# Choosing the weight pieces of the adding DMA by a count of the DMA engines' time instead of by fixed shares

## The chip, the cores and the metric

The kernel runs on one core of one Trainium2 chip. The metric is the device time of one execution in microseconds (us); several executions are timed and their median is given. Beside the times there is one profiled execution, whose trace holds every instruction of TensorE (PE, with its weight loads as PEld), VectorE (DVE), ScalarE (ACT), GpSimd (POOL) and SyncE (SP), and every transfer.

## The reference

The input is one sequence of 256 rows of 1024 numbers (float32). Two blocks of two layers each follow. Cut to what matters:

```python
def first_block(x, ...):
    for l in range(2):
        x = hybrid_layer(x, ...)
    return rmsnorm(x, final_norm_g)

def hybrid_layer(x, ...):
    proj = einsum("bsd,de->bse", rmsnorm(x, norm_g), w_in)          # 1024 x 3584
    (a_u, a_v, a_z, b_b, b_c, b_x, b_z, c_q, c_k, c_v, c_z, d_q, d_k, d_v, d_z) = split(proj)
    y_a = conformer_conv(a_u, a_v, ...) * silu(a_z)                 # 31-wide conv, layernorm, silu
    y_b = short_gated_conv(b_b, b_c, b_x, ...) * silu(b_z)          # 3-wide conv
    y_c = window_gqa(c_q, c_k, c_v, swa_sink) * silu(c_z)           # sliding-window attention
    y_d = neighborhood_attn(d_q, d_k, d_v, na_rpb) * silu(d_z)      # 2-D attention with a bias
    return x + einsum("bse,ed->bsd", concatenate([y_a, y_b, y_c, y_d]), w_out)

def second_block(x, ...):
    for i in range(2):
        x = x + 0.5 * _swiglu(_rmsnorm(x), ffn1_w_gate[i], ffn1_w_up[i], ffn1_w_down[i])
        x = x + _mixing(_rmsnorm(x), w_in[i], w_out[i], ...)        # two attentions and a recurrence
        x = x + 0.5 * _swiglu(_rmsnorm(x), ffn2_w_gate[i], ffn2_w_up[i], ffn2_w_down[i])
    return _rmsnorm(x, final_norm)
```

The four feed-forward networks have 1024 x 2816 gate and up matrices and a 2816 x 1024 down matrix each. All products are wanted at nearly float32 precision.

## The kernel before

**Weights and their halves.** All weights come once from memory, in 206 chunks, most of them 128 x 2048 float32 (1 MB, 16 tiles of 128 x 128, in the order in which PE uses them). A chunk is loaded into one of three buffers `st` by SP's queue (`weight_loads`). The matrix products run in fp32r, a faster form with fewer bits, so each weight is split into `hi` (the weight rounded to fp32r) and `lo` (what the rounding left), with three buffers of each; a product of the activation (split alike) with a weight tile is three matmuls. PE has two kinds of tile: in the "T" tiles (lines 563 to 565, `MM3`) the weight tile is loaded three times for 256 columns each; in the "W" tiles (lines 576, 577 and 579, `MMW`) it is two matmuls, of 512 columns with `hi` and 256 with `lo`.

**How a piece is split.** `weight_splits` takes each chunk in two halves ("pieces"; the first two chunks in four). ACT copies the piece to `hi` (profile: L472, hi<-st). Then `lo` is made in one of two ways: DVE subtracts (L495, lo<-st,hi), or ACT copies -hi into `lo` (L472, lo<-hi) and POOL issues a DMA that adds `st` onto it (L592, lo<-st), with no work for DVE. When the last piece of a chunk is done, its `st` goes back to the loads and `nprep`, the number of chunks split, is raised. `at` is the number of chunks that PE's tasks have taken. Which way a piece goes is decided before by a fixed share of the pieces in each kind of stage (line 451 and lines 628 to 630): 0.25 in the feed-forward stages (`SHARE_F`), 0.6 in the mixing stages of block 1 (`SHARE_A`), 0.45 in those of block 2 (`SHARE_B`). A counter `owed` grows by the share with every piece, and a piece that brings it to 1 is an add, from chunk 3 on (`FAST`).

**Who sets the order.** The program has no loops on the chip. In the build, `Scheduler.step` runs the tasks (generators) greedily: each pending operation has a cost in a small table of durations, each engine a clock (P, A, V, G, and D for SP's loads), each dependence between engines a latency (`LAT`); the operation with the least start time less a weighted priority goes next, onto the end of its engine's instruction stream. So the planner's numbers fix the static order of every engine, and on the chip the engines wait for each other by semaphores. Clock D is charged for a load with its bytes over 360e3 per us (`DMA`, whose duration is `nbytes / 360e3`). For an add, `DMAadd` charges POOL 1.2 us for the issue and puts the result 4.0 us later (`ADD_LATE`); D is not charged.

**Stages.** In time there are eight: the two mixing layers of block 1 (A0, A1; function `mix_a`), then for each layer of block 2 a feed-forward stage, a mixing stage (B0, B1; `mix_b`) and a feed-forward stage (ffn1 to ffn4). A feed-forward stage is 33 chunks, 528 tiles. A mixing stage A is two chunks for the values (v0, v1), then 13 groups of projections in the order a_v, a_u, b_c, c_z, c_q, c_k, d_z, d_q, b_z, b_x, d_k, b_b, a_z (a chunk each, c_k half a one; T tiles), then the output projection (4 chunks, W tiles) over y. Chunk 3 is a_u, chunk 4 b_c, chunk 6 c_q. Behind a_u, DVE makes `hp` and from it `ca`, the 31-wide convolution, in 62 steps, and a layernorm follows: PE sums over the channels (`ca,ones`), ACT takes the mean, DVE subtracts it, and so on, up to `a_z` and the first two row groups of y. The second attention (`na`, twice) begins with the scores (`dk,dq` on PE) and the bias step of the softmax on DVE (L526), which needs the bias `nb`, gathered by eight SP transfers of 96 KB from `rpb` (task `biases`, per mixing layer). The short convolution is `bp` and `bc`. The first y groups that the output projection wants are those of the two attentions, its last those of the two convolutions.

## Time and profile before

| | |
|---|---|
| median of 3 runs | 1361.81 us (1359.84, 1361.81, 1370.74) |
| the profiled execution | 1359.77 us, span of its instructions 1358.0 us, mean granted TensorE clock 0.978 |
| PE busy | 1277.9 us, 94% (weight loads 1144.4 us, 84%) |
| DVE busy | 865.0 us, 64% |
| ACT busy | 921.3 us, 68% |
| POOL busy | 320.1 us, 24% |
| HBM | 217.94 MB read, 1.05 MB written |

The span runs from the first to the last instruction of the profiled execution; 1.8 us of its time lie around it. A matmul's end is modelled and matmuls overlap their weight loads, so a busy PE isn't PE at its peak; the granted clock (PEclk, 1.00 is the higher of TensorE's two levels, 2.4 GHz, and 0.50 the lower, 1.2 GHz) says at which speed it ran. "DMA share" is the mean busy share of the core's 16 DMA engines. The stages are read from the trace at A0 4 to 152 us, A1 152 to 290, ffn1 290 to 478, B0 478 to 634, ffn2 634 to 820, ffn3 820 to 1006, B1 1006 to 1160, ffn4 1160 to 1358. In a row of a group or of the timeline, "bank<-act,hi" is what an instruction writes and reads, [5.84 <-DMA lo<-st] how long it stood before and what it waited for; "xN" the number of instructions.

### The profile page before, as it was taken

How to read it: one execution, taken by the hardware profiler on the slowest of the kernel's cores; microseconds unless marked ns; L12 is line 12 of the kernel's file. 1: busy time of each engine (PE TensorE's matmuls, PEld its weight loads, DVE VectorE, ACT ScalarE, POOL GpSimd, SP SyncE). 2: the span in 40 equal slices, each digit the busy share in tenths (PEclk: the TensorE clock that was granted, in tenths of full speed). 3: DMA queues.
4: the chain of work that ended last, by engine and by line, in shares of the span. 5: the costliest groups of instructions: out<-in, count | busy, mean ns of one | idle time of the engine just before them, and what ended most of it. 6: DMA issues, size and time to landing. Idle time of an engine off the chain costs nothing.

```text
span 1358.0 us, 21863 instructions
## 1 busy us (share of the span) xinstructions
PE 1277.9 (94%) x8530; PEld 1144.4 (84%) x8530; DVE 865.0 (64%) x1481; ACT 921.3 (68%) x1420; POOL 320.1 (24%) x318
## 2 busy tenths in 40 slices
PE   6899988999999999789999999999999888999997
PEld 5888887888888898678888888888899776888886
DVE  6586658569966556856666556666555785666632
ACT  5487748777686578587666656666559767766652
POOL 4222312242121112512222112222121340322211
PEclk9899998999999999899999999999999899999998
DMA  8887988798777779255877777777778645877771
GB/s 262 229 234 203 231 237 232 204 241 271 224 235 240 236 219 256 82 171 156 263 233 234 228 230 228 225 240 237 239 232 230 180 104 161 236 243 242 236 226 53
DMA packets 59783, 294.09 MB, mean 217 GB/s; under 512 B 12448, under 2 KB 14240, under 8 KB 34208
## 3 DMA queue, kind: packets, MB, share of 16 engines
q1 hardware_dynamic: 39232, 219.01, 45.3%
q0 software_dynamic: 20448, 73.69, 28.5%
q8 instruction: 67, 1.10, 0.3%
q14 instruction: 36, 0.29, 0.1%
HBM read 217.94 MB, written 1.05 MB: 161 GB/s over the span
## 4 chain that ended last, share of the span: by engine, by line
PE 70%; ACT 10%; DVE 7%; DMA 7%; issue 3%; POOL 2%; SPq 0%; POOLq 0%; DVEq 0%; ACTq 0%
PE bank L576 34%; PE bank L577 19%; PE bank L579 4%; DMA lo<-st 3%; DVE sp L495 3%; ACT hi L472 3%; DMA st<-ws 3%; PE bank L563 2%; PE bank L565 2%; PE bank L564 2%; ACT lev L472 2%; PE bank L535 2%; ACT lo L472 1%; PE bank L546 1%; ACT pt L472 1%
## 5 line engine op out<-in xcount | busy, mean ns | idle before, releaser
L576 PE MATMUL bank<-act,hi 128*128 128x512 f32 x1456 | 520.0, 395 | 2.3 <-DVE act L495 2.3
L472 ACT ACTIVATE hi<-st 128x1024 fp32r<-128x1024 f32 (+3 forms) x416 | 428.6, 1036 | 80.6 <-DMA st<-ws 39.2
L577 PE MATMUL bank<-act,lo 128*128 128x256 f32 x1664 | 433.4, 281 | 0.6 <-ACT act L472 0.6
L495 DVE TENSOR_TENSOR lo<-st,hi 128x1024 fp32r<-128x1024 f32 (+1 forms) x274 | 338.0, 1237 | 133.5 <-ACT hi L472 130.1
L577 PEld LDWEIGHTS bank<-act,lo 128*128 128x128 f32 x1664 | 312.8, 188 | 18.6 <-ACT act L472 0.9
L576 PEld LDWEIGHTS bank<-act,hi 128*128 128x128 f32 x1456 | 273.6, 188 | 57.8 <-DVE act L495 3.8
L592 POOL DMA_DIRECT2D lo<-st x142 | 123.9, 873 | 652.2 <-ACT lo L472 524.1
L576 PE MATMUL bank<-ha,hi 128*128 128x512 f32 x672 | 236.7, 394 | 0.0
L565 PE MATMUL bank<-act,lo 128*128 128x256 f32 x720 | 208.9, 290 | 24.9 <-DMA lo<-st 24.9
L563 PE MATMUL bank<-act,hi 128*128 128x256 f32 x720 | 214.1, 297 | 0.0
L564 PE MATMUL bank<-act,hi 128*128 128x256 f32 x720 | 207.7, 288 | 0.0
L577 PE MATMUL bank<-ha,lo 128*128 128x256 f32 x704 | 192.7, 281 | 0.0
L565 PEld LDWEIGHTS bank<-act,lo 128*128 128x128 f32 x720 | 141.7, 197 | 26.1 <-DMA lo<-st 26.1
L472 ACT ACTIVATE lo<-hi 128x1024 fp32r<-128x1024 f32 (+1 forms) x142 | 149.3, 1052 | 3.8
L576 PEld LDWEIGHTS bank<-ha,hi 128*128 128x128 f32 x672 | 126.2, 188 | 27.0
L563 PEld LDWEIGHTS bank<-act,hi 128*128 128x128 f32 x720 | 142.1, 197 | 5.9 <-issue 5.0
L564 PEld LDWEIGHTS bank<-act,hi 128*128 128x128 f32 x720 | 141.4, 196 | 0.1
L577 PEld LDWEIGHTS bank<-ha,lo 128*128 128x128 f32 x704 | 132.4, 188 | 2.7
L495 POOL TENSOR_TENSOR fs<-fs,rbc 128x512 f32<-128x512 f32 x44 | 64.0, 1456 | 179.4 <-ACT fs L472 179.4
L495 DVE SCALAR_TENSOR_TENSOR x<-bank,x 128x256 f32<-128x256 f32 x128 | 53.6, 422 | 58.6 <-PE bank L579 56.7
L495 DVE TENSOR_TENSOR fh<-bank,fh 128x256 f32<-128x256 f32 x88 | 37.1, 423 | 76.6 <-ACT fh L472 76.6
L579 PE MATMUL bank<-act,hi 128*128 128x512 f32 x208 | 82.2, 395 | 0.1
(216 smaller groups left out, 1543.8 us busy)
## 6 DMA issues: line engine op xcount, KB each, us to landing
st<-ws SPq DMA_DIRECT2D x197, 1024.0 KB, 5.0
lo<-st POOLq DMA_DIRECT2D x136, 512.0 KB, 5.7
st<-ws SPq DMA_DIRECT2D x2, 1040.0 KB, 7.1
st<-ws SPq DMA_DIRECT2D x4, 512.0 KB, 7.4
st<-ws SPq DMA_DIRECT2D x8, 192.0 KB, 5.3
nb<-rpb SPq DMA_DIRECT2D x16, 96.0 KB, 7.5
st<-ws SPq DMA_DIRECT2D x2, 768.0 KB, 6.5
lo<-st POOLq DMA_DIRECT2D x2, 520.0 KB, 6.7
```

The lines of the kernel that those rows point to most:

```text
L472: return Op([("A", dur, lambda: self.nc.scalar.activation(out, in_, func, **kw))], outs, ins, ACT_SETS.get(func))
L495: return (eng, dur, lambda: fn(out, *ins, **kw)), [extent(a) for a in aps]
L535: return Op([("P", dur, lambda: self.nc.tensor.matmul(out, lhsT, rhs, start=start, stop=stop))], [extent(out)], [extent(lhsT), extent(rhs)])
L546: mm(o, l, r, start=st, stop=sp)
L563: mm(out, ah, bh, start=first, stop=False)
L564: mm(out, ah, bl, start=False, stop=False)
L565: mm(out, al, bh, start=False, stop=last)
L576: mm(out, wh, x, start=first, stop=False)
L577: mm(out[:, 0], wl, x[:, 0], start=False, stop=False)
L579: mm(out, wh, x, start=False, stop=True)
L592: return Op([("G", ADD_ISSUE, lambda: self.nc.gpsimd.dma_start(out, src, accum_op=ALU.add))], [extent(out)], [extent(src), extent(out)], l ...
```

## The change

`owed`, `share` and the three fixed shares go. In their place the planner now charges an add to clock D as well: an operation has `moves`, the free size of the piece times `ADD_RATE` (2.7e-3 us for each of 1024 elements of a partition, so 2.76 us), which begins when both D and POOL's issue are done and moves D on; the result is there 1.9 us after that (`ADD_LATE`). A piece becomes an add when three things hold at the moment its `hi` copy has been placed: the chunk is 3 or later, as before; at least one chunk more has been split than PE's tasks have taken (`nprep > at`); and the planner's clock D is not ahead of ACT's (`c["D"] <= c["A"]`).

```diff
@@ -206,18 +206,16 @@
 PRIO = dict(w1=0.8, w2=-1.8, w3=0.4, epilogue=0.5, gate=1.7, up=1.5, rstd=2.0, norm=1.3, values=0.7,
             conv=0.3, att=1.8, evac=1.1, level=0.3, prep=-0.7, rec=2.3, bias=-1.3, vg=0.2)
 ADD_ISSUE = 1.2
-ADD_LATE = 4.0
-SHARE_F = 0.25
-SHARE_A = 0.6
-SHARE_B = 0.45
+ADD_LATE = 1.9
+ADD_RATE = 2.7e-3
 WEIGH = dict(P=0.0118, A=0.7, V=0.35, G=0.1681, D=1.0)
 
 
 class Op:
-    __slots__ = ("ways", "outs", "ins", "tset", "dep", "gen", "late")
-
-    def __init__(self, ways, outs, ins, tset=None, late=0.0):
-        self.ways, self.outs, self.ins, self.tset, self.late = ways, outs, ins, tset, late
+    __slots__ = ("ways", "outs", "ins", "tset", "dep", "gen", "moves")
+
+    def __init__(self, ways, outs, ins, tset=None, moves=0.0):
+        self.ways, self.outs, self.ins, self.tset, self.moves = ways, outs, ins, tset, moves
 
 
 class Event:
@@ -385,7 +383,10 @@
         w[2]()
         end = start + cost
         self.clock[eng] = end
-        self.commit(op, eng, end + op.late)
+        if op.moves:
+            self.clock["D"] = end = max(self.clock["D"], end) + op.moves
+            end += ADD_LATE
+        self.commit(op, eng, end)
         t.op = None
         self.advance(t)
         return True
@@ -448,7 +449,6 @@
         self.used = 0
         self.nprep = 0
         self.at = 0
-        self.share = self.owed = 0.0
 
 
     def A(self, out, in_, func, scale=1.0, bias=0.0, accum_out=None):
@@ -590,7 +590,7 @@
     def DMAadd(self, out, src):
 
         return Op([("G", ADD_ISSUE, lambda: self.nc.gpsimd.dma_start(out, src, accum_op=ALU.add))],
-                  [extent(out)], [extent(src), extent(out)], late=ADD_LATE)
+                  [extent(out)], [extent(src), extent(out)], moves=free_n(src) * ADD_RATE)
 
     def split(self, hi, lo, src):
         yield self.A(hi, src, AF.Copy)
@@ -625,9 +625,8 @@
                 s = slice(j * n // parts, (j + 1) * n // parts)
                 yield self.loaded[i][j]
                 yield self.A(hi[:, s], st[:, s], AF.Copy)
-                self.owed += self.share
-                self.owed, on_pool = (self.owed - 1.0, True) if self.owed >= 1.0 else (self.owed, False)
-                if on_pool and i >= FAST:
+                c = self.s.clock
+                if i >= FAST and self.nprep > self.at and c["D"] <= c["A"]:
                     yield self.A(lo[:, s], hi[:, s].bitcast(F32), AF.Copy, scale=-1.0)
                     yield self.DMAadd(lo[:, s].bitcast(F32), st[:, s])
                 else:
@@ -952,7 +951,6 @@
                 yield nxt["summed"][KT - 1]
                 done.done = True
 
-            self.share = SHARE_F
             s.spawn(self.rstd(st, "copy"), PRIO["rstd"])
             if extra is not None:
                 s.spawn(extra, 0.0)
@@ -1274,7 +1272,6 @@
                 yield nxt["summed"][KT - 1]
                 done.done = True
 
-            self.share = SHARE_A
             s.spawn(self.rstd(st, "both"), PRIO["rstd"])
             s.spawn(norm(), PRIO["norm"])
             s.spawn(self.free_rows(st, True))
@@ -1694,7 +1691,6 @@
                 yield nxt["summed"][KT - 1]
                 done.done = True
 
-            self.share = SHARE_B
             s.spawn(self.rstd(st, "normed"), PRIO["rstd"])
             s.spawn(norm(), PRIO["norm"])
             s.spawn(self.free_rows(st, False))
```

The build gives these numbers of adds on POOL, by stage:

| | A0 | A1 | ffn1 | B0 | ffn2 | ffn3 | B1 | ffn4 | all |
|---|---|---|---|---|---|---|---|---|---|
| before | 20 | 22 | 18 | 15 | 18 | 16 | 15 | 18 | 142 |
| changed | 7 | 10 | 18 | 13 | 19 | 20 | 14 | 26 | 127 |

The first add is in chunk 3 (a_u, both halves) before and in chunk 6 (c_q, its first half) in the changed kernel. In the feed-forward stages most chunks have an add in one half; before it is mostly the first half, in the changed kernel mostly the second.

The orders of the engines change with it. Where a buffer's name carries a number, the number is the buffer's alone.

On SP, in the front of A0, the order before; `st` is a weight chunk, `nb` the bias of the second attention, `msk` a mask that is needed late:

```order
L587 DMA st_73<-ws 128x2048
L587 DMA nb<-rpb 64x6x64 x3
L587 DMA st_71<-msk 128x384
L587 DMA nb<-rpb 64x6x64 x5
L587 DMA st_71<-ws 128x2048
```

and in the changed kernel:

```order
L587 DMA st_73<-ws 128x2048
L587 DMA st_71<-ws 128x2048
L587 DMA st_72<-msk 128x384
L587 DMA nb<-rpb 64x6x64 x8
L587 DMA st_72<-ws 128x1024
```

The load of chunk 6 (the `st_71<-ws` row) stood behind the eight gathers and now stands ahead of them.

On ACT, at the same place, the order before; hi_75 and lo_78 are chunk 4, hi_76 and lo_79 chunk 5, hi_74 and lo_77 chunk 6, and a row lo<-hi is the negated copy of an add:

```order
L472 ACTIVATE hi_75<-st_72 128x1024 x2
L472 ACTIVATE lo_78<-hi_75 128x1024
L472 ACTIVATE hi_76<-st_73 128x1024 x2
L472 ACTIVATE lo_79<-hi_76 128x1024
L472 ACTIVATE hi_74<-st_71 128x1024
L472 ACTIVATE lo_77<-hi_74 128x1024
```

and in the changed kernel (act is the activation, xnt a normed row group on the way into it):

```order
L472 ACTIVATE hi_75<-st_72 128x1024
L472 ACTIVATE act_81<-xnt_88 128x2x256
L472 ACTIVATE hi_75<-st_72 128x1024
L472 ACTIVATE act_81<-xnt_89 128x2x256
L472 ACTIVATE hi_76<-st_73 128x1024 x2
L472 ACTIVATE hi_74<-st_71 128x1024
L472 ACTIVATE lo_77<-hi_74 128x1024
```

The negated copies of chunks 4 and 5 are gone; that of chunk 6's first half stays and is the first of the program.

On PE, at the end of A0's projections, the order before; dk and dq are the second attention's operands, and rows L563 to L565 are a T tile of a projection:

```order
L546 MATMUL bank_120<-dk,dq 128x256
L546 MATMUL bank_123<-dk,dq 128x256
L563 MATMUL bank_117<-act_81,hi_75 128x256
L564 MATMUL bank_117<-act_81,hi_75 128x256
L565 MATMUL bank_117<-act_81,lo_78 128x256
```

and in the changed kernel (rows L576 and L577 are a W tile of the output projection; ca, th and dg belong to the convolution's layernorm):

```order
L565 MATMUL bank_118<-act_81,lo_79 128x256
L576 MATMUL bank_119<-act_80,hi_74 128x512
L577 MATMUL bank_119<-act_80,lo_77 128x256
L535 MATMUL bank_123<-ca,ones 128x256 x2
L576 MATMUL bank_119<-act_80,hi_74 128x512
L577 MATMUL bank_119<-act_80,lo_77 128x256
L535 MATMUL bank_123<-ones,th_159 128x1 x4
L535 MATMUL bank_123<-dg_114,ones 128x128
L535 MATMUL bank_123<-dg_115,ones 128x128
L546 MATMUL bank_122<-dk,dq 128x256
L546 MATMUL bank_121<-dk,dq 128x256
```

Before, 61 T tiles stand behind ca,ones and 37 behind the last of the scores (dk,dq); in the changed kernel both stand behind the last T tile, with one W tile ahead of ca,ones and one behind it. In A1 of the changed kernel half of the scores stands ahead of the last 33 T rows and the other half has 8 tiles behind it.

## Rows read from the trace of the kernel before

**Rows 1.** DMA queues of the page: packets, MB, share of 16 engines' span
```profile
q1 hardware_dynamic: 39232, 219.01, 45.3%
q0 software_dynamic: 20448, 73.69, 28.5%
```

**Rows 2.** Busy time by stage: A0, A1, ffn1, B0 and ffn4
```profile
core 0: us, PE busy (x) PEld busy (x) DVE busy (x) ACT busy (x) POOL busy (x), PEclk, DMA share, GB/s
4.00:152.00 148.00, 128.06 (x906) 117.75 (x906) 105.34 (x232) 101.24 (x173) 45.06 (x56) 0.95 0.87 237
152.00:290.00 138.00, 123.74 (x900) 114.88 (x899) 91.06 (x218) 97.38 (x161) 33.40 (x41) 0.96 0.88 226
290.00:478.00 188.00, 187.28 (x1082) 164.06 (x1081) 135.39 (x226) 131.80 (x190) 40.62 (x43) 1.00 0.78 242
478.00:634.00 156.00, 137.63 (x1205) 126.72 (x1204) 103.39 (x175) 114.86 (x198) 43.54 (x32) 0.96 0.61 168
...
1160.00:1358.00 198.00, 189.68 (x1096) 166.01 (x1094) 105.09 (x150) 118.46 (x169) 37.88 (x37) 0.98 0.68 207
```

**Rows 3.** Waits in A0, A1, B0: us in total, times, longest
```profile
PE bank L565 <- DMA lo<-st: 11.8, 2, 6.0
...
PE bank L565 <- DMA lo<-st: 13.0, 4, 6.0
...
PE bank L553 <- DVE pt L495: 5.6, 2, 5.4
```

**Rows 4.** PE's timeline at A0's first wait (start, duration), and what follows
```profile
33.56 0.58 PE L565 MATMUL bank<-act,lo 128*128 128x256 f32 x1 [5.84 <-DMA lo<-st]
34.00:40.00 6.00, 6.00 (x31) 6.00 (x31) 2.15 (x3) 4.50 (x5) 1.98 (x3) 0.52 0.84 148
```

**Rows 5.** Adds' time to landing in A0, then ffn1; the chain at 25:60
```profile
DMA to landing us min/median/max: 4.0/5.7/13.0
...
DMA to landing us min/median/max: 4.7/5.4/8.9
...
35.22 2.88 DMA nb<-rpb
38.09 12.97 DMA lo<-st
```

**Rows 6.** Groups of the page: busy, mean ns | idle before, releaser
```profile
L495 DVE TENSOR_TENSOR lo<-st,hi 128x1024 fp32r<-128x1024 f32 (+1 forms) x274 | 338.0, 1237 | 133.5 <-ACT hi L472 130.1
L472 ACT ACTIVATE lo<-hi 128x1024 fp32r<-128x1024 f32 (+1 forms) x142 | 149.3, 1052 | 3.8
```

**Rows 7.** A0's timeline of DVE and PE, with the busy times of 42:98
```profile
42.08 0.69 DVE L495 TENSOR_TENSOR hp<-th,bank 128x512 f32<-128x512 f32 x1 [0.54 <-PE bank L565]
42.00:98.00 56.00, 47.35 (x369) 44.69 (x368) 44.13 (x110) 37.33 (x64) 11.29 (x13) 0.94 0.88 248
95.50 2.06 DVE L495 SCALAR_TENSOR_TENSOR ca<-hp,cw,ca 128x256 f32<-128x256 f32 x5
98.22 1.02 PE L535 MATMUL bank<-ca,ones 128*128 128x256 f32 x4
113.76 0.42 DVE L526 CUSTOM_DVE_ANT_0 pt<-bank,nb 128x256 f32<-128x256 f32 x1
125.57 0.76 DVE L495 TENSOR_TENSOR act<-y,act 128x256 fp32r<-128x256 f32 x2
```

**Rows 8.** Timelines and busy times: A0's output projection, A1's hp and output projection
```profile
129.69 0.40 PE L576 MATMUL bank<-act,hi 128*128 128x512 f32 x1
188.37 0.68 DVE L495 TENSOR_TENSOR hp<-th,bank 128x512 f32<-128x512 f32 x1
188.00:236.00 48.00, 39.42 (x291) 36.80 (x292) 42.68 (x110) 34.13 (x61) 8.82 (x10) 0.89 0.88 235
236.00:273.00 37.00, 36.38 (x282) 33.20 (x282) 22.39 (x59) 28.49 (x52) 8.49 (x10) 1.00 0.80 205
267.97 0.39 PE L576 MATMUL bank<-act,hi 128*128 128x512 f32 x1
```

## The prediction

> **What bounds the kernel now.** I read the busy times by stage first. A feed-forward (FFN) stage is TensorE alone: PE is busy 187.28 of 188 us, clock 1.00 [rows 2], 528 weight tiles at 0.355 us, and nothing waits. So its mixture of adds and subtractions is free as long as each piece is there in time. The two mixing stages of block 1 (A0, A1) differ: PE is busy 128.06 of 148 and 123.74 of 138 us, the DMA share is 0.87 and 0.88, and the clock averages 0.95 and 0.96. The table of waits, read next for these two, says what PE stands for: lo pieces that an adding DMA brings, 11.8 us in two waits and 13.0 in four [rows 3]. PE's timeline shows the second price: after 5.84 us of idleness it goes on at a granted clock of 0.52 for six microseconds [rows 4], which is the lower of its two levels, 1.2 GHz, and costs about 3 us more. In the mixing stages of block 2 (B0, B1) PE also stands, but for DVE's pt in the attention (5.6 us [rows 3]); their DMA share is 0.61 [rows 2].
>
> The adds are slow in A0 because the queues are full: 5.7 us from issue to landing in the median and up to 13.0, against 5.4 and 8.9 in the first FFN [rows 5]. The worst one lands 12.97 us after its issue, behind the gather of the attention bias (nb<-rpb) [rows 5].
>
> **The change, part by part.** *Counts.* From POOL's order: adds by stage were 20, 22, 18, 15, 18, 16, 15, 18 and become 7, 10, 18, 13, 19, 20, 14, 26; in all 142 becomes 127. One add costs ACT 1.05 us for the negated copy, one subtraction costs DVE 1.24 us [rows 6]. A queue's share of the span, times 1358 us, gives what the transfers take of the 16 engines: 45.3% over 219.01 MB is 2.95 us for a 1.05 MB weight chunk; 28.5% over 142 adds is 2.7 us each [rows 1].
>
> *Stage A0, what is released.* Thirteen adds fewer free 13 x 2.7 = 35 us of DMA of the 148 x 0.87 = 129 us there. The first add is now in chunk 6 (c_q), so the two long PE waits, in a_u and b_c, have nothing to wait for: 11.8 us, and with them two stretches at half clock, 3 us each. At most 17.8 us. What remains in front: c_q's first half is still an add, and its ACT copies come just when all eight gathers of nb stand in SP's queue (the SP and ACT rows of the change). Before, such an add took 13 us, and PE arrives about 5 to 8 us after this one's issue: bounds 0 and 8 us, I take 2, as half the DMA traffic around it is gone.
>
> *Stage A0, what takes its place.* The thirteen pieces go to DVE, which also runs the 62-step convolution on ca. Before, it ran from hp at 42.08 to its last ca step at 97.56; DVE was busy 44.13 of the 56 us from 42 to 98 [rows 7]. By DVE's order the same stretch will hold 15 whole and 2 half lo pieces instead of 5 and one half: 10.5 x 1.24 = 13.0 us more, plus the short convolution bp/bc and the splits of y that were behind it, about 5.5 us. hp itself comes earlier, at about 39 (before it DVE has 4 pieces more but no DMA to wait for). 39 + 44.1 + 13.0 + 5.5 = 101.6 us: four microseconds later than before, where PE would like to be 18 us earlier. The planner knows this and moves the consumers: in PE's new order the mean of ca and the whole second attention (dk,dq) stand behind the last projection, with two weight tiles between them, where 61 tiles stood behind ca,ones before. PE gets there at 27.7 (where it stopped for the first add [rows 4]) + 184 tiles x 0.355 + about 7 us of the first attention + 3 us of waits = 103. From there the chain is bare. The trace has its length: ca,ones at 98.22, bias step of the softmax at 113.76, split of y at 125.57 to 126.3 [rows 7]; 28 us, of which about 6 were DVE's and PE's other work. I take 21.5 us (bounds 18 and 28). So the output projection starts at about 124.5, where it started at 129.69 [rows 8]; two of its tiles are already done, and some 2.5 us go to a low clock after a stretch in which PE works 9 of 21 us. Net gain of A0: 129.7 - 124.5 + 0.7 - 2.5 = 3.4 us; bounds -5 (28 us and 8 us of c_q) and +12.
>
> The row for that last charge is the one already named: 5.84 us idle, then clock 0.52 [rows 4]. The Trainium skill ("TensorE: Matmul & The Clock Gate", Part 1) says it as a rule against this change: the throttled state is the default and only activity releases it. By it the bare chain is charged at its end, which gives the 3.4; without it A0 would gain 5.9. The trace agrees at the two waits of A0; no row shows a bare chain of this length.
>
> *Stage A1.* Twelve adds fewer. PE's four waits, 13.0 us, and about 3 us of half clock are released: 16 at most. Here the planner keeps cover: half of the second attention stands before the last 29 tiles. DVE has room: from hp at 188.37 [rows 8] it was busy 42.68 of 48 and 22.39 of 37 us [rows 8], 20 us free, and gets 7 whole and one half piece more, 9.3 us. Three of the four waits lie ahead of hp, so hp comes earlier with PE. The second half of the attention has only 8 tiles behind its scores; I charge 3 to 4 us of wait there. Net gain 12, bounds 5 and 16: the output projection from 267.97 [rows 8] to about 256 on the old scale.
>
> *B0, B1.* Two adds and one fewer: 2.5 and 1.2 us on DVE, hidden in the 34% of the span in which DVE is idle there (103.39 busy of 156 [rows 2]). But PE's order changes around the levels of the recurrence: some get more T tiles behind them, three get none. Each level can win or lose a wait of about 2 us: 0, bounds -6 and +6.
>
> *FFNs.* Adds stay at 18 to 20 in three of them and rise to 26 in the last: 33 x 2.95 + 26 x 2.7 = 168 us of DMA against 186 of PE. Hidden; ACT gets 8 x 1.05 = 8.4 us on top of 118.46 busy of 198 [rows 2]. Most adds move from a chunk's first half to its second, which PE needs half a chunk, 2.8 us, later. Loss 0, bound 6.
>
> *POOL* loses fifteen issues, about 1 us each, and was waiting. *SP* loads wait for st to come free; pieces split on DVE free it without a landing of 5.4 us.
>
> *Sum.* 1359.8 (the profiled execution: span 1358.0 and 1.8 around it) - 3.4 - 12 + 0 = 1344.4; I write 1345. The three runs before have a median of 1361.8, their lower two 1359.8 and 1361.8, so the profiled one is typical.
>
> A price that only a page has: the Trainium skill ("DMA: Bandwidth & Descriptors", Anatomy of one DMA) fits 2.0 us plus bytes over 436e3, 3.2 us for half a megabyte. By it the planner's 1.2 + 2.8 + 1.9 would be cautious, and c_q's 2 us would be none: 1343. The rows disagree: 5.4 us even in the FFN.
>
> **The rivals.** (1) *Both A stages gain.* If DVE's back-to-back pieces cost less than their 1.24 us (they overlap) and the chain is nearer 18 us, A0 gives 12 and A1 16: 1332. For it: DVE's idle time. Against: the chain's own links. (2) *DVE eats both.* The load that left the DMA sits on the engine that feeds the attention; if A1's chain is as bare as A0's, A1 gives 5 and A0 loses 3: about 1358. For it: the planner's own move of ca,ones behind everything. (3) *The change doesn't do what it says.* The count charges a 96 KB gather by its bytes, 0.27 us, though eight of them were followed by landings of 13 us [rows 5]. Then c_q's add costs its upper bound of 8 us instead of 2, with 3 us of half clock behind it, and A1's first add 2 us: 1345 + 11 = 1356, within 1% too. (4) *Slower: the last FFN.* Where nearly every chunk has one add, load and add need 2.95 + 2.7 = 5.65 us of DMA for 16 x 0.355 = 5.68 us of PE. It decides from the point where an add lands later than about 9 us after its issue (8.9 was the longest in the first FFN [rows 5]); then st is freed late, the next load too, and PE stands. Ten such chunks with 2 us each, and half clock after the longer ones, cost 30 us: 1375. Against it: the rule itself places an add only when the count is behind ACT, and the share would be 0.9, about that of A0, where not every add was late.
>
> **How the numbers follow.** Forecast 0.50, (1) 0.13, (2) 0.22, (3) 0.07, (4) 0.08. The forecast's own range is 1334 to 1356 (A0's and A1's bounds do not all fall together). The range that leaves out 2 in 10 reaches from 1331, just past (1), to 1362, past (2) and (3) but short of (4). Faster by over 1% (below about 1347; 1% is what a measurement of this kernel can tell from no change): 0.43 of the forecast's 0.50 and all of (1), 0.56. Within 1%: 0.07 of the forecast, (2) and (3), 0.36. Slower 0.08.
>
> **What would show it.** In the profile after: no PE wait on lo<-st of 6 us in the front of A0 (right) or one in c_q (rival 3); DVE busy over 0.8 of A0; PE standing some 12 us near the end of A0 on ACT or DVE of the conv's norm and the attention, with clock 0.5 after it; A1 shorter by 9 to 16 us with DMA share near 0.7; FFN stages at 186 to 188 us each. The prediction is wrong if A0 is shorter by more than 12 us, if A1 is not, or if an FFN grows.

## The result, and the profile after

The changed kernel's median is 1371.0 us (1363.61 to 1378.86, 14 runs), that of the kernel before, measured beside it, 1362.76 us (1359.68 to 1370.74, 14 runs): a ratio of 1.0061, interval 1.0036 to 1.0085. It is slower by 0.6%, some 8 us; the forecast was 1345, in a range of 1331 to 1362. The profiled execution took 1370.33 us, with a span of 1368.6. Stage lengths, here and below, are from one profiled execution of each kernel. Where two kernels have the same order of instructions in a stage they still differ by up to 4 us (A0: 138.0 in front_nb and 141.8 in front_none, below), so smaller differences of one stage show nothing by themselves.

| stage, us of the span | before | after | difference | forecast |
|---|---|---|---|---|
| A0 | 148 | 153.0 | +5.0 | -3.4 (bounds -12, +5) |
| A1 | 138 | 127.7 | -10.3 | -12 (bounds -16, -5) |
| ffn1 | 188 | 195.8 | +7.8 | 0 (bound +6 for all four) |
| B0 | 156 | 155.4 | -0.6 | 0 |
| ffn2, ffn3 | 186, 186 | 185.8, 186.7 | -0.2, +0.7 | 0 |
| B1 | 154 | 153.9 | -0.1 | 0 |
| ffn4 | 198 | 206.3 | +8.3 | 0 |
| sum | | | +10.6 | -15.4 |

POOL's queue on the page, against [rows 1]: 15 adds fewer and 7 MB less.

```profile
q0 software_dynamic: 18288, 66.48, 25.4%
```

Busy time by stage (columns as in [rows 2]): A0, A1, ffn1, ffn2, ffn4, and in the last row 42 us of ffn4.

```profile
4.00:157.00 153.00, 130.98 (x906) 117.87 (x906) 118.99 (x245) 88.27 (x158) 34.30 (x42) 0.93 0.63 193
157.00:284.70 127.70, 120.50 (x902) 111.50 (x901) 106.27 (x230) 84.90 (x150) 30.44 (x33) 1.00 0.66 195
284.70:480.50 195.80, 189.81 (x1084) 163.98 (x1082) 133.31 (x222) 131.73 (x188) 43.17 (x43) 1.00 0.76 228
635.90:821.70 185.80, 185.80 (x1072) 162.91 (x1070) 108.31 (x152) 120.23 (x169) 40.61 (x39) 1.00 0.80 237
1162.30:1368.60 206.30, 190.75 (x1093) 165.02 (x1092) 97.55 (x141) 123.77 (x175) 44.30 (x45) 0.99 0.80 224
...
1234.00:1276.00 42.00, 37.98 (x215) 32.30 (x214) 21.29 (x31) 29.27 (x42) 9.43 (x10) 1.00 0.93 245
```

The adds did what was asked of them in the two A stages: the DMA share fell from 0.87 and 0.88 to 0.63 and 0.66. DVE is now busy 118.99 of 153 us in A0, where it was 105.34 of 148. In ffn1 PE stands 6 of 195.8 us, in ffn4 15.5 of 206.3; before it was 0.7 of 188 and 8.3 of 198. ffn4's mean DMA share is 0.80, no more than that of ffn2, where PE never stands. But for 42 us of it the share is 0.93.

Where the adds stand matters below. In the program of the kernel before about half of the chunks of a feed-forward stage have one, not most of them: behind the first two or three chunks it is every other chunk. The changed kernel puts adds into runs of neighbouring chunks, the longest of five in ffn1, four in ffn2, seven in ffn3, and eight and ten in ffn4.

The waits of ffn1, ffn4 and A1 (us in total, times, longest):

```profile
PE bank L577 <- DMA lo<-st: 5.7, 7, 1.8
...
PE bank L577 <- DMA lo<-st: 7.2, 6, 2.2
...
PE bank L576 <- DVE act L495: 3.0, 1, 3.0
PE bank L565 <- DMA lo<-st: 0.9, 1, 0.9
```

The first two account for 13 us, where the feed-forward stages lost 16.6: PE waits in short pieces for halves that an adding DMA brings. In A1 the 13.0 us of such waits [rows 3] are down to 0.9.

A0's timeline, PE from the first weight wait to the output projection, then DVE:

```profile
51.41 0.58 PE L565 MATMUL bank<-act,lo 128*128 128x256 f32 x1 [5.73 <-DMA lo<-st]
...
111.75 1.02 PE L535 MATMUL bank<-ca,ones 128*128 128x256 f32 x4
115.80 1.02 PE L535 MATMUL bank<-ones,th 128*128 128x1 f32 x8 [2.68 <-ACT th L472]
...
120.38 3.79 PE L546 MATMUL bank<-dk,dq 64*128 64x256 f32 x16
135.36 0.50 PE L576 MATMUL bank<-act,hi 128*128 128x512 f32 x1 [1.60 <-DVE act L495]
...
38.49 0.68 DVE L495 TENSOR_TENSOR hp<-th,bank 128x512 f32<-128x512 f32 x1
109.51 1.67 DVE L495 SCALAR_TENSOR_TENSOR ca<-hp,cw,ca 128x256 f32<-128x256 f32 x4
122.50 0.42 DVE L526 CUSTOM_DVE_ANT_0 pt<-bank,nb 128x256 f32<-128x256 f32 x1 [1.25 <-PE bank L546]
```

One wait for an add is left, in c_q, of 5.73 us. The convolution's last step ends only at 111.2. The bare chain follows (layernorm, scores, and the bias step pt, which waits for the scores), and the output projection starts at 135.36 (before: 129.69 [rows 8]).

### The profile page after: what moved, and what is told of

It is laid out like the page before. It is cut to its first block, busy times and chain, and to the rows that moved or that the text cites. A ratio compares the mean times of both kernels' runs of the same rounds, so it can differ in the third digit from the quotient of the medians.

```text
span 1368.6 us, 21842 instructions
## 1 busy us (share of the span) xinstructions
PE 1280.2 (94%) x8530; PEld 1139.4 (83%) x8530; DVE 883.8 (65%) x1492; ACT 899.5 (66%) x1404; POOL 315.9 (23%) x307
## 4 chain that ended last, share of the span: by engine, by line
PE 58%; DVE 12%; ACT 11%; DMA 10%; issue 6%; POOL 1%; SPq 1%; DVEq 0%; POOLq 0%; ACTq 0%
PE bank L576 23%; PE bank L577 13%; DMA lo<-st 9%; PE bank L563 4%; PE bank L565 4%; PE bank L564 4%; ACT hi L472 3%; DVE sp L495 3%; DVE lo L495 3%; PE bank L579 2%; PE bank L546 2%; ACT lev L472 2%; ACT lo L472 2%; DMA st<-ws 1%; PE bank L553 1%
## 5 line engine op out<-in xcount | busy, mean ns | idle before, releaser
L576 PE MATMUL bank<-act,hi 128*128 128x512 f32 x1456 | 520.4, 395 | 6.1 <-DVE act L495 6.1
L472 ACT ACTIVATE hi<-st 128x1024 fp32r<-128x1024 f32 (+3 forms) x416 | 423.4, 1033 | 103.5 <-DMA st<-ws 70.3
L577 PE MATMUL bank<-act,lo 128*128 128x256 f32 x1664 | 434.8, 281 | 9.1 <-DMA lo<-st 9.1
L495 DVE TENSOR_TENSOR lo<-st,hi 128x1024 fp32r<-128x1024 f32 (+3 forms) x289 | 356.8, 1244 | 124.9 <-ACT hi L472 124.7
L577 PEld LDWEIGHTS bank<-act,lo 128*128 128x128 f32 x1664 | 312.8, 188 | 31.2 <-DMA lo<-st 13.9
L576 PEld LDWEIGHTS bank<-act,hi 128*128 128x128 f32 x1456 | 273.6, 188 | 60.7 <-DVE act L495 7.8
L592 POOL DMA_DIRECT2D lo<-st x127 | 110.9, 873 | 587.3 <-ACT lo L472 363.0
L576 PE MATMUL bank<-ha,hi 128*128 128x512 f32 x672 | 236.9, 394 | 0.0
L565 PE MATMUL bank<-act,lo 128*128 128x256 f32 x720 | 206.0, 286 | 10.6 <-DMA lo<-st 10.5
L563 PE MATMUL bank<-act,hi 128*128 128x256 f32 x720 | 211.5, 294 | 0.0
L564 PE MATMUL bank<-act,hi 128*128 128x256 f32 x720 | 205.3, 285 | 0.5 <-DVE act L495 0.5
L577 PE MATMUL bank<-ha,lo 128*128 128x256 f32 x704 | 193.2, 282 | 5.0 <-DMA lo<-st 5.0
L576 PEld LDWEIGHTS bank<-ha,hi 128*128 128x128 f32 x672 | 126.2, 188 | 26.8
L565 PEld LDWEIGHTS bank<-act,lo 128*128 128x128 f32 x720 | 138.8, 193 | 11.7 <-DMA lo<-st 11.7
L563 PEld LDWEIGHTS bank<-act,hi 128*128 128x128 f32 x720 | 139.0, 193 | 4.6 <-issue 3.8
L577 PEld LDWEIGHTS bank<-ha,lo 128*128 128x128 f32 x704 | 132.4, 188 | 9.4 <-DMA lo<-st 6.6
L564 PEld LDWEIGHTS bank<-act,hi 128*128 128x128 f32 x720 | 138.7, 193 | 1.0 <-DVE act L495 0.7
L472 ACT ACTIVATE lo<-hi 128x1024 fp32r<-128x1024 f32 (+1 forms) x127 | 134.3, 1057 | 3.2
```

The source lines that it names most:

```text
L472: return Op([("A", dur, lambda: self.nc.scalar.activation(out, in_, func, **kw))], outs, ins, ACT_SETS.get(func))
L495: return (eng, dur, lambda: fn(out, *ins, **kw)), [extent(a) for a in aps]
L563: mm(out, ah, bh, start=first, stop=False)
L564: mm(out, ah, bl, start=False, stop=False)
L565: mm(out, al, bh, start=False, stop=last)
L576: mm(out, wh, x, start=first, stop=False)
```

## The experiments

Two theories about the two losses.

**Feed-forward stages.** *Theory:* an add holds its `st` buffer until it lands. With an add in every neighbouring chunk the three buffers come back later than PE wants one (16 tiles x 0.355 = 5.68 us a chunk), although the mean DMA share is below 1. *Rival:* the half matters (PE wants the second half at once), or ACT's negated copies.

**A0.** *Theory:* c_q's add makes PE late. *Rival:* DVE is late by itself, with the convolution or with the scaling of `nb`, which the scores stand behind.

In all the diffs `rule` stands for the changed kernel's condition without `i >= FAST`, and `k` is the number of a chunk within its feed-forward stage, or None:

```python
k = next((i - a for a in (38, 89, 122, 173) if 0 <= i - a < 33), None)
```

### Which density of adds a feed-forward stage bears (ladder, ladder_st4)

The changed kernel with a fixed place for the adds in each of the four stages: second halves of every second chunk (17 adds), first halves of all chunks (33), second halves of all (33), 26 spread evenly over the halves.

```diff
+ if k is not None:
+     add = (k % 2 == 0 and j == 1 if i < 71 else j == 0 if i < 122 else j == 1 if i < 155
+            else (2 * k + j + 1) * 26 // 66 > (2 * k + j) * 26 // 66)
```

> The changed kernel with the adds of the feed-forward stages put by hand: ffn1 one in the second half of every other chunk (17), ffn2 one in the first half of every chunk (33), ffn3 one in the second half of every chunk (33), ffn4 26 spread evenly over the 66 halves. Stage times before were 188, 186, 185 and 198 us. Theory (st): what counts is how many neighbouring chunks hold their buffer for an add; ffn1 stays at 186 to 188, ffn2 and ffn3 need about 6.4 us a chunk once the lead is used up, 200 to 206 us each, ffn4 203 to 207 as in the changed kernel. Rival (half): the second half is what hurts, since st is then freed later; ffn1 and ffn3 grow by 7 us and more, ffn2 stays at 186. Rival (DMA): the DMA engines' work is the bound, a load and an add each 5.65 us; ffn2 and ffn3 are then 187 to 192 us.

ladder_st4 is the same with a fourth `st` buffer; its room is taken from `sq`, `lev` and `pt`, which have one buffer fewer.

```diff
- slots("st", 3, [P, WMAX])
+ slots("st", 4, [P, WMAX])
```

> The ladder (17, 33, 33, 26 adds in the four feed-forward stages, placed alike) with four st buffers for three; to make room, three other buffers that the mixing stages of block 2 and the sums use are one fewer each, so the mixing stages may be longer and are not compared. The ladder's stages took 187.9, 213.5, 221.2 and 211.7 us. Theory (st): the time for which an add holds a buffer was the bound; with four buffers ffn2 and ffn3 fall to the work of the DMA engines, 33 times 5.65 to 5.95 us, 187 to 197 us, and ffn4 to 198. Rival (DMA): the transfers themselves are the bound and a fourth buffer only lets more of them collide; ffn2 and ffn3 stay within 5 us of 213 and 221, ffn4 of 212.

Busy time of ffn1 to ffn4 with three buffers:

```profile
285.80:473.70 187.90, 187.70 (x1083) 164.32 (x1081) 133.07 (x223) 126.11 (x183) 43.15 (x42) 1.00 0.73 226
629.60:843.10 213.50, 195.08 (x1071) 167.34 (x1069) 93.08 (x139) 137.40 (x188) 52.84 (x53) 0.97 0.93 247
843.10:1064.40 221.30, 196.07 (x1072) 167.09 (x1070) 94.29 (x140) 132.09 (x181) 48.39 (x49) 0.97 0.87 237
1220.00:1431.70 211.70, 193.36 (x1093) 167.59 (x1091) 96.82 (x141) 124.55 (x176) 45.78 (x46) 0.97 0.77 215
```

and of ffn2 to ffn4 with four (ffn1 took 189.8):

```profile
626.40:829.70 203.30, 191.78 (x1072) 164.86 (x1070) 93.77 (x139) 133.66 (x185) 52.53 (x53) 0.98 0.94 255
829.70:1037.30 207.60, 194.06 (x1072) 167.41 (x1070) 93.11 (x137) 132.81 (x182) 50.13 (x51) 0.97 0.90 247
1189.40:1388.80 199.40, 189.32 (x1093) 165.20 (x1091) 95.21 (x141) 125.40 (x177) 44.51 (x45) 0.98 0.78 219
```

The whole kernels took 1433.44 and 1390.62 us, one execution each. With three buffers, seventeen adds in every second chunk cost nothing (PE busy 187.70 of 187.9). Twenty-six, often in neighbouring chunks, cost ffn4 13.7 us (211.7 against 198) at a share of only 0.77. Thirty-three cost 27 us in first halves (ffn2) and 35 in second ones (ffn3): the half may matter, but it is by far the smaller part. The fourth buffer gives ffn4 12.3 of its 13.7 us back, ffn2 and ffn3 10 and 14. ACT's negated copies are the same with three buffers and four, so they aren't what the 12.3 us were lost to. What is left there has a share of 0.94 and 0.90, and the DMA engines themselves are the likely bound. So in the stage with 26 adds it is the time for which a buffer is held, not the amount moved, that costs. The plan was made anew for four buffers, so the engines' orders differ too; the fourth buffer is not the only difference between the two runs.

### Fixed places in the feed-forward stages (ffn_fixed, lead8)

ffn_fixed is the changed kernel with the add in the first half of every second chunk, 17 in each stage:

```diff
+ add = rule if k is None else k % 2 == 0 and j == 0
```

> The changed kernel, but in the four feed-forward stages an add goes to the first half of every other chunk (17 per stage), as before; the mixing stages keep the new rule. Theory (st): in the changed kernel ffn1 and ffn4 lost 7.5 and 8.7 us because the rule puts adds into six to eight neighbouring chunks; such a chunk holds its st buffer 14 to 25 us, the three buffers then come back less than once in the 5.68 us in which PE uses a chunk up, and the next load is late. By it the four stages come back to 186 to 188 us (the last to 198), the mixing stages stay at 152, 128, 155 and 154, and the whole at about 1353 us, ratio 0.994 to before. Rival (plan): the loss is from the other engines' new orders under the new durations of the plan; then the feed-forward stages keep their 7 to 9 us and the time stays near 1370.

Measured 1369.46 us, ratio 1.0047 (1.0029 to 1.0065): a miss, and no gain over the changed kernel that is clear of noise (1.0061). Its profiled execution was its fastest, 1363.7, with ffn1 191.6, ffn2 189.1 and ffn4 199.2, so ffn1 and ffn2 still lose some 3 us each. A likely reason stands in the landing times. Before, from 675 to 760 (busy row, then issue to landing of the adds and of the loads):

```profile
675.00:760.00 85.00, 85.00 (x490) 74.50 (x489) 53.07 (x76) 58.63 (x85) 18.60 (x16) 1.00 0.78 239
DMA to landing us min/median/max: 4.5/4.6/5.0
DMA to landing us min/median/max: 4.7/4.8/5.1
```

and ffn_fixed from 690 to 770, the same pattern of adds:

```profile
690.00:770.00 80.00, 79.71 (x453) 68.65 (x451) 52.31 (x71) 51.60 (x77) 14.44 (x13) 1.00 0.78 230
DMA to landing us min/median/max: 5.7/9.5/10.5
DMA to landing us min/median/max: 4.7/5.3/10.4
```

The same share, 0.78, and adds that take 4.6 us or 9.5 in the median. In the first way load and add follow each other with little overlap. In the second a load waits until the add ahead of it lands and sets a buffer free; then two loads are issued almost together and the next add about a microsecond behind them: at 701.8, 702.2 and 703.0 us, landing after 5.1, 10.4 and 10.5 us. Six of the seven adds take 9.1 to 10.5 us, and the load just ahead of each of them 8.8 to 10.4; the other load of the round takes about 5. The late add again frees its buffer late, which is why this can last; it is read from the issue and landing times, and no run tests it alone. In this stretch PE stands only 0.3 us, but its weight loads wait three times for an add, 1.5 us in all, which they never do in the stretch of the kernel before: the splits have no lead left that could cover a delay. The Trainium skill ("DMA: Bandwidth & Descriptors", Queues, rings and completion order) says that a DMA engine takes turns between the queues that have work for it; that the second load and the add, which stand in two queues, land within 0.9 to 2.0 us of each other agrees with it.

lead8 has no adds in the first eight chunks of a stage, so that a lead can form first, and moves up the scaling of `nb` (nb_early, below):

```diff
+ add = rule if k is None else k >= 8 and k % 2 == 0 and j == 0
```

> The changed kernel with nb prepared early, and in the feed-forward stages no add in the first eight chunks, then one in the first half of every other (13 per stage); the mixing stages keep the new rule. In the run ffn_fixed, with adds in every other chunk from the first on, ffn3 ran with all its lead (186 us, loads 4.8 and adds 5 to 7 us) while ffn1 and ffn2 ran 20 to 30 chunks with none (191 and 189 us, loads and adds of 9 to 10 us side by side). Theory (lead): a stage that starts without a lead of split chunks falls into the second of two steady states, in which transfers collide and the lead never comes back; eight chunks without an add restore it, and all four stages take 186, 186, 186 and 198 us; with A0 at 143 the whole is about 1341 us. Rival (plan): it is the order of the engines under the new durations that makes the transfers collide, so ffn1 and ffn2 stay at 189 to 192 us and the whole is 1350.

1362.63 us, ratio 1.0004 (0.9989 to 1.0018). ffn2 to ffn4 took 187.0, 185.4 and 199.9. ffn1 still took 195.2, without adds in its first eight chunks. By estimate some 3 us of that are the clock: it was granted at 0.51 from 288 to 293 us and at 0.86 from 293 to 300, where the changed kernel has 1.00 from 284.7 on. From 354.9 to 363.6 no load was issued, with ACT busy 5.93 and DVE 5.67 of the 6 us from 358 to 364; PE then waited 2.1 us for an add. So adds aren't the only cause of a lost lead. That they are why it stays lost was not tested.

### No adds in the feed-forward stages (after_none, before_f0)

The changed kernel with none there:

```diff
- if i >= FAST and rule:
+ if i >= FAST and k is None and rule:
```

> The changed kernel with no adds in the feed-forward stages (no other edit). Theory (any add): every loss there, 7.5, 0, 1.3 and 8.7 us against the kernel before, hangs on adds that run beside loads; without adds the stages take 187, 186, 185.5 and 198 us and the whole about 1353 us, ratio 0.993, which is the change's gain in A1 less its loss in A0. Rival (plan): ffn1 loses because of its order under the new durations (in lead8 and gap it took 195 and 200 us with 13 and 14 adds only), and stays above 192 us without any add; the whole is 1360 or more.

and the kernel before with `SHARE_F = 0.0`:

> The kernel before with the share of the feed-forward stages at 0 for 0.25 (no other edit). In its profile these stages took 188, 186, 185 and 198 us, near what TensorE needs, but its times spread from 1359 to 1371 us, and in front_nb, with the same share, ffn2 took 190. Theory (any add): some executions of the kernel before lose a few us in the feed-forward stages too; without adds the median falls by 2 to 7 us, to 1356-1360. Rival (none): the kernel before loses nothing there, and the median stays at 1361 to 1364; what front_none gained over front_nb came from B0 (149 for 156 us) and the like.

after_none: 1361.92 us, ratio 0.9982 (0.9962 to 1.0001). Busy rows of its ffn1 and ffn4:

```profile
287.10:476.60 189.50, 189.19 (x1084) 165.53 (x1082) 154.27 (x241) 115.08 (x172) 27.54 (x25) 0.99 0.52 185
1161.80:1361.10 199.30, 190.47 (x1093) 166.72 (x1091) 124.41 (x167) 102.01 (x154) 25.11 (x21) 0.97 0.44 158
```

The two stages are 6.3 and 7.0 us shorter, all four 12.0 of the 16.6 lost, and PE stands 0.3 us in ffn1. DVE does all the subtractions and is busy 154.27 of 189.5: it has the room. The median falls by 9 us against the changed kernel's, half of the 18 that were expected, and the ratios' intervals lie apart: the adds there do cost the changed kernel time. No waits for adds can be left in these stages. The other 5 us are for the most part the clock: it was granted at 0.66 from 292 to 297 us (ffn1), 0.75 from 638 to 643 (ffn2) and 0.74 from 1167 to 1172 (ffn4), 4 us in all by estimate, where the kernel before has 1.00 at the start of these stages.

before_f0: 1352.74 us, ratio 0.9936 (0.9911 to 0.996), more than expected. Its feed-forward stages took 188.7, 186.3, 185.4 and 196.8, as before. The largest difference in its profile is B0 with 149.0 instead of 156; why B0 gains from a share that isn't its own stays open. The counter `owed` carries what is left of it from stage to stage, so that B0 has 13 adds for 15 and another order, and PE stands 11.7 us there for 18.4.

Beside before_f0, which has only eight adds left in these stages, after_none shows what the count does elsewhere: its span is 11 us longer, with A0 +5.6, A1 -7.8, B0 +7.0 and the others +6. So the changed kernel's loss isn't the adds of the feed-forward stages alone.

### What holds A0 (no_cq, nb_early, nb_nocq)

no_cq: the changed kernel without c_q's add, all else alike.

```diff
- if i >= FAST and rule:
+ if i > 6 and rule:
```

> The changed kernel with no add before chunk 7, so that the wait of 5.9 us for c_q's add in A0 and the half clock behind it (3 us) have nothing to come from; the add moves to chunks 8 and 9. Theory (PE late): PE's arrival at the last projection tile sets when the bare chain of A0 begins; A0 shrinks from 152 to 143 us and the whole from 1371 to 1362. Rival (DVE late): ca is done on DVE at 111.2 us, when PE's last tile is, and DVE was busy from 98 to 107 without a gap; then PE only arrives earlier and waits at ca, A0 shrinks by 2 to 4 us, and the whole is about 1368.

nb_early: the changed kernel, but the scaling of the bias `nb` gets a high priority once it is gathered.

```diff
- s.spawn(biases(), PRIO["bias"])
+ s.spawn(biases(), lambda: PRIO["bias"] if "nb" not in box else 1.3)
...
+ box["nb"] = True      # in biases(), behind the gathers
```

> The changed kernel with one more edit: once the gathers of nb are issued, DVE's and POOL's preparation of nb gets a high priority in the plan (1.3 for -1.3). In the changed kernel DVE scales nb at 115 to 119.6 us, long after its landing, and the scores of the second attention stand behind the last projection; here DVE scales it right behind hp, and the scores stand some 30 tiles ahead of the end. Theory (nb late): A0's bare chain is the late nb, and A0 shrinks from 152 to about 143 us, the whole to about 1362 (the feed-forward stages still lose their 16 us, ffn1 has 23 adds here). Rival (conv late): the layernorm behind the convolution ends the chain anyway, done on DVE at 111 us; A0 stays at 149 to 152, the whole at 1368 to 1371.

nb_nocq: both.

> The changed kernel with nb prepared early (as in nb_early) and no add before chunk 7 (as in no_cq). Alone, the first took A0 from 152 to 147.6 us, with 5.9 us of waiting for c_q's add and 5 us at the output projection left in it; the second alone left A0 at 153. Theory (two in a row): c_q's wait was hidden behind the late nb; without both, A0 falls to 138-141 us. Rival (conv late): what ends A0 now is the convolution on DVE, whose share of A0 is 0.81; A0 stays at 145 to 148 us. The feed-forward stages keep their losses (23, 19, 24 and 26 adds), so the whole stays near 1360.

no_cq: 1370.39 us, ratio 1.0053 (1.0033 to 1.0074), and A0 still 153.0 us long: the 5.73 us wait is gone (one of 2.2 us for a later add stands in its place), and nothing is won. The rival has the cause right, though not its 2 to 4 us: PE is through with the last T tile at 106.9 us and then waits 2.15 us for ca, which ends on DVE at 110.3, 0.9 us earlier than in the changed kernel. The output projection begins at 134.53, 0.8 us earlier, and runs its first 3.8 us at the lower clock level:

```profile
134.50:138.30 3.80, 3.77 (x12) 3.24 (x13) 0.43 (x1) 0.10 (x1) 0.00 (x0) 0.51 0.00 0
```

The scaling of `nb` on DVE (tile nb; times in ns, then from when to when) was done by 98.8 in the A0 of before (first row); in the changed kernel (second) and in no_cq (third) it stands behind the convolution. The bias step pt did not wait for it there but for the scores on PE (1.25 us in the changed kernel), which the plan had put behind the layernorm:

```profile
L495 DVE TENSOR_SCALAR nb<-nb x4: 354/358/1107, 39.9 to 98.8; 128x384 f32<-128x384 f32 x4
...
L495 DVE TENSOR_SCALAR nb<-nb x4: 347/353/614, 114.9 to 119.3; 128x384 f32<-128x384 f32 x4
...
L495 DVE TENSOR_SCALAR nb<-nb x4: 347/353/1147, 110.2 to 113.2; 128x384 f32<-128x384 f32 x4
```

Busy time of A0 in nb_early, where c_q's wait is 5.8 us, and in nb_nocq:

```profile
4.90:152.50 147.60, 128.19 (x903) 117.06 (x903) 119.25 (x241) 87.05 (x155) 36.30 (x44) 0.93 0.65 200
...
4.80:148.00 143.20, 127.57 (x902) 116.34 (x902) 118.94 (x244) 86.69 (x155) 34.34 (x41) 0.93 0.66 205
```

Alone, the earlier `nb` gives 5.4 us of A0; without c_q's wait it gives 9.8. (With the changed kernel's order in A0, ffn_fixed and after_none took 150.7 and 152.1; with that of nb_early, lead8 took 146.9. So the first gain is 3 to 6 us.) The two latenesses hide each other: c_q's wait is worth nothing while `nb` is late, and 4.4 us when it is early, one execution each. The convolution ends later in both, at 122.3 and 117.6 us for 111.2. Little of the gain reaches the median. A1 grows to 131.5 and 133.1 us, for 127.7 to 130.1 in the changed kernel, ffn_fixed and after_none; and nb_early's plan has 12 adds more, five of them in ffn1 and four in ffn3, which grew to 192.9, while ffn4 stayed at 207.3. nb_early took 1372.9 us, ratio 1.0076 (1.0051 to 1.0101), nb_nocq 1368.84 in its only execution.

### The old shares in the mixing stages (mix_fixed)

The changed kernel, its rule in the feed-forward stages, the old 0.6 and 0.45 elsewhere:

```diff
+ if k is None:
+     self.owed += 0.6 if i < 38 else 0.45
+ add = rule if k is not None else self.owed >= 1.0
+ if k is None and add:
+     self.owed -= 1.0
```

> The other half: the new rule in the feed-forward stages alone, the fixed shares 0.6 and 0.45 in the mixing stages (20, 22, 17 and 16 adds), all in the new cost model of the plan. The feed-forward stages get 16, 6, 20 and 21 adds, with runs of six neighbouring chunks in ffn1 and of five at the end of ffn3 and ffn4. Theory (st): ffn1 loses about 6 us in its run, ffn2 nothing, ffn3 1 us and ffn4 2 us; A0 and A1 have the waits of the kernel before again (147 and 138 us), a little more in A0, since the plan puts the scores of the second attention behind the last projection: about 1370 us. Rival (plan): the feed-forward stages lose as much in ffn2 as in ffn1, whatever the runs, and the whole is 1375 or more.

1426.6 us, ratio 1.0458 (1.0412 to 1.0504), which no theory had: A0 166.5 us and A1 170.4. Its A0 is not that of the kernel before: the adds there go by the same shares, but the plan has the new numbers, in which an add is charged to D. The waits of A0 and A1, and the gathers of `nb` on SP's queue:

```profile
PE bank L554 <- DVE pt L496: 23.5, 2, 22.0
...
PE bank L554 <- DVE pt L496: 30.2, 3, 28.9
...
L588 SPq DMA_DIRECT2D nb<-rpb x8: 617/850/1841, 69.0 to 132.8; - x8
```

Twenty adds put twenty charges of 2.76 us on the planner's D, the clock on which the gathers with their low priority are planned too. They are issued from 69.0 to 132.8 us, where the changed kernel issues them from 33.3 to 38.0, and the second attention waits 22 us; in A1 they come as late (224.3 to 300.6). Since the selection in A0 and A1 is that of the kernel before, the harm is in the planner's new numbers; that it is the charge, and not the shorter `ADD_LATE`, is argued from the gathers and was not tested apart.

### Versions that take only what helped (front_nb, gap, front_none, front_f0)

front_nb is the kernel before, with its fixed shares but no adds in the first chunks of A0 and A1, and the earlier `nb`:

```diff
- if on_pool and i >= FAST:
+ if on_pool and i >= FAST and not (i < 8 or 19 <= i < 28):
```

> The kernel before, with its fixed shares and its old durations in the plan, and two edits: no add before chunk 8 in A0 and before the ninth chunk of A1 (14 and 12 adds there for 20 and 22), and nb prepared early as in nb_early. It takes from the change what helped (no add where PE waits for it in the front of A0 and A1) without the count. Theory: A0 loses its two waits of 6 us and the half clock behind them and gets 7 us more on DVE, 147 to 135-138 us; A1 goes to 128 as in the changed kernel; the feed-forward stages keep their 186 and 198: about 1342 us, ratio 0.985. Rival (DVE late): the convolution is what A0 waits for, A0 stays at 145 to 147 us, and the whole is 1350 to 1352.

gap is nb_nocq with never two adds in neighbouring chunks, 66 adds in all:

```diff
+ if i > 6 and self.last < i - 1 and rule:
+     self.last = i
```

> The changed kernel with three repairs: nb prepared early, no add before chunk 7, and no add in a chunk whose neighbour before it has one. The count then places 66 adds (127 in the changed kernel), 14, 4, 13 and 5 in the feed-forward stages. Theory: with A0 at about 140, A1 at 130, the feed-forward stages at 188, 186, 186 and 198 and the others at 155, the whole is about 1342 us, ratio 0.985. Rival (DVE late): the 61 pieces more, 1.24 us each, are too much for DVE in A0 and A1, whose convolution waits for them; A0 147, A1 135, and the whole 1352 to 1356.

front_none is front_nb with `SHARE_F = 0.0`, front_f0 the same without the earlier `nb`.

> The run front_nb (1347.2 us) with no adds at all in the feed-forward stages but for the few whose pieces are split ahead of them. Its stages took 188, 190, 186 and 198 us with 18, 18, 16 and 18 adds. Theory (an add there buys nothing): DVE has 0.57 to 0.72 of these stages and takes some 16 pieces more, 20 us, without being late; loads fly alone, the lead never goes, and the four stages take 187, 186, 185.5 and 198: about 1341 us. Rival (DVE): DVE becomes late for the pieces in ffn1, where it is busiest; ffn1 grows by 3 us and more, and the whole is 1347 or more.

> The run front_none (1333 us) without its early nb: before's shares, no adds in the feed-forward stages and none in the first chunks of A0 and A1. Here the plan puts nb's preparation behind most of the convolution, and half of the second attention's scores behind A0's last projection, as the count did. Theory (nb late): A0 is 148 to 152 us for 141.8, and the whole 1340 to 1343. Rival (conv late): A0 stays within 3 us of 141.8, and the whole of 1333.

front_nb: 1347.18 us, ratio 0.9881 (0.9861 to 0.9901). gap: 1359.28, 0.9977 (0.9955 to 0.9999), a miss of 17 us. front_none: **1333.03 us, 0.9799 (0.9766 to 0.9832)**, the fastest of all. front_f0: 1339.13, 0.9827 (0.9797 to 0.9857).

Busy rows: A0 and A1 of front_nb, ffn1 of gap, A0 of front_none, A0 of front_f0.

```profile
4.90:142.90 138.00, 125.67 (x903) 114.68 (x902) 112.59 (x238) 92.60 (x162) 40.36 (x48) 0.98 0.81 238
142.90:271.10 128.20, 122.52 (x901) 113.33 (x900) 101.29 (x226) 90.22 (x153) 30.56 (x35) 0.97 0.74 206
...
283.40:483.00 199.60, 192.79 (x1083) 166.57 (x1082) 139.20 (x228) 127.18 (x184) 39.18 (x39) 0.98 0.70 213
...
4.90:146.70 141.80, 126.84 (x903) 115.01 (x903) 112.78 (x238) 92.66 (x162) 40.40 (x48) 0.96 0.79 230
...
4.90:146.90 142.00, 126.52 (x901) 114.38 (x901) 113.12 (x239) 93.39 (x162) 38.70 (x47) 0.98 0.79 232
```

So the forecast's gain in the A stages, and more, is there to be had: take the adds from the front alone, prepare `nb` early and leave the rest of the mixture. A0 of front_nb is 10 us shorter than before and A1 9.8, with a DMA share still at 0.81 and 0.74, and DVE has 6 us less to do in A0 than in the changed kernel. front_none has the same order in A0 and took 141.8 there, and 142.0 without the earlier `nb` (front_f0): here the earlier `nb` shows no gain. The medians of these two are 6 us apart, but their intervals overlap and the profiled executions took 1335.56 and 1335.34, so no difference between them is shown. What front_none has over front_nb is not all in the feed-forward stages either: B0 took 149.4 for 155.8, as in before_f0.

gap missed in three stages. A0 and A1 took 145.7 and 132.8 for the 140 and 130 expected, near the rival (DVE late), and ffn1 199.6 for 188, with its 14 adds at every other chunk or rarer. By estimate some 3 us of ffn1 are the clock (0.71 from 288 to 293 us, 0.95 from 293 to 330); the rest goes with the overlapping transfers: from 344 to 443 us its adds, then its loads, and PE's wait; at 448 to 483, where the lead is back, the same two again.

```profile
DMA to landing us min/median/max: 5.5/8.8/11.6
DMA to landing us min/median/max: 4.7/5.5/11.1
  PE bank L577: 4.8, 5
...
DMA to landing us min/median/max: 4.5/5.0/5.5
DMA to landing us min/median/max: 4.8/4.9/7.3
```

## Why the prediction was wrong

Two of its terms carried the error: the feed-forward stages, put at 0, came to +16.6 us, and A0, put at -3.4, came to +5.0. A1, B0 and B1 were close.

**The FFN step** failed at "33 x 2.95 + 26 x 2.7 = 168 us of DMA against 186 of PE. Hidden". This is an average over a stage, and what decides is a run of neighbouring chunks. In the row of 1234 to 1276 the share is 0.93, and a chunk takes 42 us x 16 x 2 / 215 = 6.3 us, for 5.68. The buffers show the same: the six loads issued from 1228.7 to 1257.0 us have their buffer loaded anew after 15.1 to 25.3 us, 19.3 in the mean, and a third of that is 6.4 us a chunk. Taking the adds out gives 6.3 of the 7.8 us of ffn1 and 7.0 of the 8.3 of ffn4 back (after_none), and in ladder_st4 a fourth buffer gives 12.3 of 13.7 back. The premise ahead of that step, that the mixture is free "as long as each piece is there in time", was taken from one execution: in front_nb, with the same shares, ffn2 took 190.2 us. Rival (4) had the mechanism, but only for ffn4 and for 30 us; the loss was 8.3 there, and 7.8 in ffn1, which has as many adds as before. That its 1375 lies near the 1371 is partly luck: half of its 30 us came, in four stages, and A0 made up for much of the rest. Its threshold, an add that lands later than 9 us, isn't borne out: from 1234 to 1276, where PE stood 4.0 us, the adds took 6.3 us in the median and 9.4 at most, and from 1180 to 1234, where PE was busy 53.95 of 54 us, 8.9 and 10.3.

**A0, what is released**: right. The two waits of 11.8 us are gone, hp came at 38.49 (forecast 39). c_q's add was mis-sized: PE waited 5.73 us, where the bounds were 0 and 8 and 2 was taken.

**A0, what takes its place**: DVE and the bare chain were the right places. What failed is the sum "39 + 44.1 + 13.0 + 5.5 = 101.6 us". It adds up DVE's work from hp to the last ca step, and the work was sized right: 61.94 us busy for 62.6. But it puts the time in which DVE stands at nothing, and that was 10.75 us, so the last ca step ended at 111.2. The row of this stretch, DVE's two longest waits in it, and what ACT waited for ahead of the first:

```profile
38.49:111.18 72.69, 64.37 (x514) 61.85 (x513) 61.94 (x133) 42.67 (x70) 8.41 (x9) 0.95 0.68 203
...
47.10 1.29 DVE L495 TENSOR_TENSOR lo<-st,hi 128x512 fp32r<-128x512 f32 x2 [4.77 <-ACT hi L472]
61.94 0.69 DVE L495 TENSOR_TENSOR th<-bank,cst 128x512 f32<-128x512 f32 x1 [3.28 <-ACT th L472]
...
46.44 1.15 ACT L472 ACTIVATE hi<-st 128x512 fp32r<-128x512 f32 x2 [6.06 <-DMA st<-ws]
```

The first wait is for the half chunk c_k, whose load now stands behind the eight gathers in SP's queue. The prediction saw the gathers there and charged them to c_q's add only. The second, with shorter ones about it 5 us in all, follows PE's wait for c_q's add. In no_cq the first is still there (6.08 us) and the second is not; hp comes 1.9 us later and ca is done 0.9 us earlier. So the convolution is late without c_q's add too.

PE reached the last T tile at 111.4, not 103. Of these 8.4 us 3.7 are c_q's, some 2.6 the clock behind that wait (granted at 0.60 from 51.4 to 58), and the other 2 shorter waits; no_cq shows that nothing is gained when PE arrives earlier. The chain took 23.6 us (111.75 to 135.36), within its bounds, 2.1 more than taken. (In the kernel before 28 T tiles stood behind the scores, not 37; in the changed one none do.)

**A0, the low clock** charged at the chain's end wasn't paid there:

```profile
120.00:137.00 17.00, 13.65 (x60) 8.48 (x59) 9.66 (x35) 10.13 (x29) 1.44 (x2) 0.65 0.08 31
137.00:157.00 20.00, 20.00 (x117) 17.59 (x116) 13.12 (x25) 12.37 (x23) 6.21 (x7) 1.00 0.58 161
```

The granted clock was 0.50 from 120 to 131 us, with PE busy 9.4 of 11, then 0.91 to 135.3, and 1.00 from the start of the output projection on. So here the price of the lower level lies inside the chain's 23.6 us. It need not: in no_cq the first 3.8 us of the projection ran at 0.51, which by estimate costs 1.9 us behind the chain. The rule of the Trainium skill ("TensorE: Matmul & The Clock Gate", Part 1) that the prediction weighed, that the throttled state is the default and activity releases it, agrees with both; the charge of 2.5 us was right in kind, and whether it falls inside the chain or behind it differs between these two runs. The sum of A0: the projection began 10.9 us later than forecast (135.36 for 124.5) and 2.5 us were not paid behind it, which makes the 8.4 us between -3.4 and +5.0.

**A1**: right, -10.3 against -12. Waits for adds fell from 13.0 to 0.9 us, the share to 0.66, and the wait that was charged at 3 to 4 us is there, 3.0 us for act. **B0, B1**: right, within 0.6 us, but by waits that cancel: in B0 PE's wait for pt grew from 5.6 to 10.2 us. **The sum** was right in its method: the stages' differences add up to the span's. Rival (2), that DVE eats the gain, was right for A0 and wrong for A1.
